# Hybrid decoder trunk: attention products with v in one task per head pair, residual norm on ScalarE, transposes of v and scores at other places in the weave

## The chip, the cores and the metric

The kernel runs on one core of one Trainium2 chip. The time is that of the whole program on the device, in microseconds (us). 2644.89 us is the median of three runs of the kernel before, which lie between 2642.65 and 2646.57.

## What is computed

Two layers over 2048 tokens of width 1024, all in float32. Each layer projects x at once into q, k, v, an attention gate, three gMLP parts and two branch gates. Attention is banded (128 keys before the query) with linear biases and a sink logit per head; the gMLP half normalises v_g and mixes it by position within chunks of 128.

```python
h = x @ w_in[l] + b_in[l]
q, k, v, z_a, u_g, v_g, z_g, g_a, g_g = split_columns(h)
y_a = sliding_window_attention(q, k, v, sinks[l]) * silu(z_a)
y_g = chunked_spatial_gating(gelu(u_g), gelu(v_g), ...) * silu(z_g)
merged = sigmoid(g_a) * (y_a @ w_branch_attn[l]) + sigmoid(g_g) * (y_g @ w_branch_gmlp[l])
x = layer_norm(ALPHA * x + merged @ w_out[l] + b_out[l], ln_g[l], ln_b[l])
```

There are 8 heads in 4 pairs; two heads of a pair share one 128-row tile, 64 rows each.

## The kernel before, in words

The work is cut into 2 layers x 4 groups of 512 tokens. `group(l, g, xs)` does one group of one layer. Its large products are 128x128 by 128x512, three for each block because every float32 operand is split into a rounded high part and a rest (`hilo`): high by high, high by rest, rest by high. A group has 1296 of them, all issued by the helper `mm` (L176). They come in units of 24: k, v, the four q tiles, four units for v_g, four for z_a, four for z_g, four for u, then the gates and branches, and last the output product.

Weights are split into high and rest in the first group of a layer only, by ScalarE (L135) and VectorE (L136), stored, and loaded as halves in the other groups.

Everything else is woven between these products. `side` is a queue of tasks, each a condition and an action. `step` counts the products and, each time `pace` of them have gone by, runs the task at the head if its condition holds; if it does not hold, it waits for another full `pace`:

```python
def step(w):
    count[0] += 1
    tick[0] += w
    while tick[0] >= pace[0]:
        tick[0] -= pace[0]
        if side and side[0][0]():
            side.popleft()[1]()
        else:
            tick[0] = 0.0
```

`pace` is 9 from the end of a group to the end of v_g (product 240), and 5 from there. The tasks of a group, in the order of the queue:

- `norm(b)`, four of them, left over from the group before (none for the first group): the residual norm of 128 rows as two instructions on VectorE (L645), two multiplications and additions by the norm's weights on GpSimd (L647, L648) and a store issued by GpSimd. In the very last group it runs another path, part of it on ScalarE (L637).
- a nop and four `v_task(r)`, appended after v's product, the 48th: each four transposes of 32x128 on VectorE (L346) that turn v into VT.
- 16 `s_task(c, b)`: scores of pair c and block b on TensorE (L375), bias and row maximum on VectorE (L383, L390), and after the fourth block the softmax (exponentials on ScalarE, L407; sums and scaling on VectorE, L409 to L412). The condition is that q's tile c is there and that 8 products have gone by since. q is evacuated in halves of 64 rows by ScalarE (L464) and VectorE (L465), k by L331 to L335.
- from product 240 on: `t_task(c, hf, r)`, 32 of them, each four transposes of the probabilities on VectorE (L425), and after the fourth two masks on GpSimd (L430, L432); between them 16 `pv_task(c, b)`, the products with v of one block (four products of 64 columns, eight instructions, L445). The fourth of a pair is followed by the multiplication with the gate (L451) and by `hilo` on ScalarE and VectorE. A product with v asks for 10 products since its masks were issued.
- statistics and norm of v_g (L511 to L520), mixing (L528 to L536), and in the second layer the turning of the next x (L287).

The program's order is a priority: within an engine the order of the instructions that comes out can differ from it, each instruction still waiting for what it needs. PSUM has five buffers for the large products and three for attention.

Of the kernel before, what the change touches and what calls it, by code (L numbers as in the profile page):

```python
# [10 lines left out]
AF = mybir.ActivationFunctionType  # L11
ALU = mybir.AluOpType
PSUM = bass.MemoryType.PSUM

P = 128
# [6 lines left out]
NB = T // P  # L22
HEADS = 8
NPAIR = HEADS // 2
HD = 64
# [10 lines left out]
PACE_E = 8.0  # L36
PACE_X = 8.0
T_DELAY = 45
P_DELAY = 10
LAG = 2  # L40
NEARLY = 5
# [7 lines left out]
def trunk_kernel(ctx, tc, xg, xt, wu, bcol, bvg, sinks, lngc, lnb, wsp, bsp, bout, ln_g, ln_b,  # L49
# [34 lines left out]
    def TT(shape=None):  # L84
        return tp.tile(shape or [P, T], F32, name=nm("t"), tag="t")
# [4 lines left out]
    def AT(shape=None):  # L90
        return ps_at.tile(shape or [P, T], F32, name=nm("at"), tag="at")

    def S(shape, tag):
        return small.tile(shape, F32, name=nm(tag), tag=tag)
# [57 lines left out]
    side = deque()  # L152
# [3 lines left out]
    count = [0]  # L156
# [41 lines left out]
    def hilo(dst, src, lo_engine=None):  # L198
        h, o = dst(), dst()
        act.copy(out=h, in_=src)  # L200
        (lo_engine or dve).tensor_tensor(out=o, in0=src, in1=f(h), op=ALU.subtract)
        return h, o
# [102 lines left out]
    def group(l, g, xs):  # L305
# [37 lines left out]
        def v_task(r):  # L343
            def go():
                for i in range(4):
                    dve.transpose(out=VT[32 * i:32 * i + 32, 1:, 32 * r:32 * r + 32],  # L346
                                  in_=v4[32 * r:32 * r + 32, :, 32 * i:32 * i + 32])
            return always, go
        side.append(nop)
        side.extend(v_task(r) for r in range(4))  # L350
        if l == 0 and g == 0:
            sp.dma_start(out=b8, in_=score_bias)
            pool.dma_start(out=vg_b, in_=bvg[l].partition_broadcast(P))
# [7 lines left out]
        q = {}  # L361
# [72 lines left out]
                due["p", c, hf] = count[0] + P_DELAY  # L434
            return (lambda: count[0] >= due["t", c]), go

        def pv_task(c, b):
            def go():
                A = att[c]
                if b == 0:  # L440
                    A["o"] = AT()
                po = A["o"]
                for kb in range(2):
                    for j in range(2):
                        pe.matmul(po[j * HD:(j + 1) * HD, b * P:(b + 1) * P],  # L445
                                  lhsT=VT[:, b + kb, j * HD:(j + 1) * HD],
                                  rhs=A["p"][b // 2][1 - kb][:, 2 * (b % 2) + j, :], start=kb == 0, stop=kb == 1,
                                  skip_group_check=True)
                if b == NB - 1:
                    y = TT()  # L450
                    dve.tensor_tensor(out=y, in0=po, in1=sza[c], op=ALU.mult)  # L451
                    ys[c] = hilo(Y, y)
                    del att[c]
            return (lambda: count[0] >= due["p", c, b // 2]), go

        side.extend(s_task(c, b) for c in range(NPAIR) for b in range(NB))
        pace[0] = PACE_S
        for c in range(NPAIR):
            ps = item()
            q_ = []  # L460
            for j in range(2):
                s, o = slice(j * HD, (j + 1) * HD), slice((1 - j) * HD, (2 - j) * HD)
                t = M()
                act.activation(out=t[s], in_=ps[s], func=AF.Identity, bias=bc[s, BQ + c:BQ + c + 1])  # L464
                dve.scalar_tensor_tensor(out=t[o], in0=ps[s], scalar=bc[s, BQ + c:BQ + c + 1],  # L465
                                         in1=f(t)[s], op0=ALU.add, op1=ALU.subtract)
                q_.append(t)
            q[c] = q_ + [count[0] + 8]


        hv = []
# [6 lines left out]
            hv.append(M(F32))  # L478
            dve.tensor_tensor(out=hv[b], in0=banks[b], in1=vg_b, op=ALU.add)
        flush(lambda: exps[0] == NPAIR)  # L480
        ready = []
        for c in range(NPAIR):
            for hf in range(2):
                for r in range(4):
                    side.append(t_task(c, hf, r))
                    if r % 2 and len(ready) > LAG:
                        side.append(ready.pop(0))
                ready += [pv_task(c, 2 * hf), pv_task(c, 2 * hf + 1)]
        for task in ready:
            side.extend([nop, task])  # L490
        pace[0] = PACE_T
        if l == 0 and g == 0:
            side.append(mix_consts(0))
# [110 lines left out]
        st = S([P, NB, 2, 6], "st2")  # L604
        mv = S([P, NB, 2], "mv2")
        rs = S([P, NB, 1], "rs2")
        last = l == DEPTH - 1 and g == NG - 1

        def stats(b, n):
            dve.tensor_scalar(out=rs[:, b:b + n, :], in0=mv[:, b:b + n, 1:2], scalar1=EPS, scalar2=None,  # L610
                              op0=ALU.add)
            pool.tensor_tensor(out=rs[:, b:b + n, :], in0=rs[:, b:b + n, :],  # L612
                               in1=mhalf[:, 0:n].unsqueeze(2), op=ALU.pow)

        def norm(b):
            row = g * NB + b
            dst = out[row * P:(row + 1) * P] if l == DEPTH - 1 else x1[g][:, b, :]
            if last:

                nmr = S([P, 1], "nmr")  # L620
                dve.scalar_tensor_tensor(out=nmr, in0=mv[:, b, 0:1], scalar=-1.0, in1=rs[:, b, :],
                                         op0=ALU.mult, op1=ALU.mult)
                own = [(T, D)] if b < NB - 2 else [(0, T), (T, T + 256)]
                rest = (0, T) if b < NB - 2 else (T + 256, D)

                def at(lo, hi):
                    return rt[b][lo // T][:, lo % T:(hi - 1) % T + 1], slice(lo, hi)
                for lo, hi in own:
                    r, cs = at(lo, hi)
                    dve.scalar_tensor_tensor(out=r, in0=r, scalar=mv[:, b, 0:1], in1=lg_b[:, cs],  # L630
                                             op0=ALU.subtract, op1=ALU.mult)
                for lo, hi in own:
                    r, cs = at(lo, hi)
                    dve.scalar_tensor_tensor(out=r, in0=r, scalar=rs[:, b, :], in1=lb_b[:, cs],
                                             op0=ALU.mult, op1=ALU.add)
                r, cs = at(*rest)
                act.activation(out=r, in_=r, func=AF.Identity, bias=nmr, scale=rs[:, b, :])  # L637
                pool.tensor_tensor(out=r, in0=r, in1=lg_b[:, cs], op=ALU.mult)  # L638
                pool.tensor_tensor(out=r, in0=r, in1=lb_b[:, cs], op=ALU.add)  # L639
                for h in range(2):  # L640
                    sp.dma_start(out=dst[:, h * T:(h + 1) * T], in_=rt[b][h])
                return
            for h in range(2):
                r, hs = rt[b][h], slice(h * T, (h + 1) * T)
                dve.tensor_scalar(out=r, in0=r, scalar1=mv[:, b, 0:1], scalar2=rs[:, b, :],  # L645
                                  op0=ALU.subtract, op1=ALU.mult)
                pool.tensor_tensor(out=r, in0=r, in1=lg_b[:, hs], op=ALU.mult)  # L647
                pool.tensor_tensor(out=r, in0=r, in1=lb_b[:, hs], op=ALU.add)  # L648
                pool.dma_start(out=dst[:, hs], in_=r)
# [34 lines left out]
        pace[0] = PACE_S  # L684
        if not last:
            stats(0, NB)
            side.extend((always, lambda b=b: norm(b)) for b in range(NB))
        return nxt

# [106 lines left out]
```

## Time and profile before

| | |
|---|---|
| runs | 2642.65, 2644.89, 2646.57 us, median 2644.89 |
| profiled execution | 2644.38 us, of which the span from the first to the last instruction is 2642.7 us |
| mean granted clock of TensorE | 0.989 of full speed |
| TensorE matmuls | 2579.4 us busy, 12176 instructions |
| VectorE | 1513.6 us busy, 3801 instructions |
| ScalarE | 650.2 us busy, 1266 instructions |
| GpSimd | 433.9 us busy, 448 instructions |

In the rows further down, PE is TensorE (PEld its weight loads), DVE is VectorE, ACT is ScalarE, POOL is GpSimd. L645 is line 645 of the kernel before. `y<-y,mv,rs` names the tile written and the tiles read. `x8` is a count. Busy time says how long an engine had an instruction in it; matmuls are pipelined, so that a single one's duration is longer than its distance to the next.

### The profile page before, as it was taken

What the parts mean: (1) busy time and instruction counts of PE and PEld (TensorE: products, weight loads), DVE (VectorE), ACT (ScalarE), POOL (GpSimd) and SP (SyncE); (2) the same over time, 40 slices, a digit from 0 to 9 for tenths busy, and PEclk for the clock granted to TensorE, in tenths of its full rate; (3) what the DMA queues carried; (4) which work ended last, traced back from release to release, by engine and by line L of the source; (5) the groups of instructions that cost most, each with busy time, mean ns of one, the idle gap of its engine ahead of it and who ended that gap; (6) DMA issues with size and microseconds to landing.
All of it is one profiled execution on the core that took longest, in us unless ns stands there. A gap on an engine that the chain in (4) does not pass through costs nothing. (4 is left out here: it accounts for less than half of the span.)

```text
span 2642.7 us, 32428 instructions
## 1 busy us (share of the span) xinstructions
PE 2579.4 (98%) x12176; PEld 2095.3 (79%) x12176; DVE 1513.6 (57%) x3801; ACT 650.2 (25%) x1266; POOL 433.9 (16%) x448
## 2 busy tenths in 40 slices
PE   8999999999999999999989999999999999999997
PEld 6788877888778887788877888778887788877886
DVE  7963478213782137824689577872467724676114
ACT  4432223211321113211144332321103211041110
POOL 1110031100311003110032100310013200121002
PEclk9999999999999999999999999999999999999999
DMA  8788954457544575456676897545665456644554
GB/s 320 238 288 291 336 208 160 165 196 260 177 159 175 192 256 189 164 187 224 249 253 207 299 322 285 177 159 189 214 228 179 161 187 211 228 173 157 181 197 164
DMA packets 116108, 568.39 MB, mean 215 GB/s; under 512 B 12112, under 2 KB 28528, under 8 KB 60528
## 3 DMA queue, kind: packets, MB, share of 16 engines
q1 hardware_dynamic: 109776, 546.35, 58.5%
q0 software_dynamic: 6176, 19.97, 2.2%
q8 instruction: 96, 1.57, 0.2%
q14 instruction: 60, 0.49, 0.1%
HBM read 436.25 MB, written 130.02 MB: 214 GB/s over the span
## 5 line engine op out<-in xcount | busy, mean ns | idle before, releaser
L176 PE MATMUL mm<-x,w 128*128 128x512 f32 x6528 | 1562.5, 396 | 10.1 <-ACT x L200 8.6
L176 PEld LDWEIGHTS mm<-x,w 128*128 128x128 f32 x6528 | 1221.5, 190 | 285.0 <-issue 21.9
L176 PE MATMUL mm<-y,w 128*128 128x512 f32 x1536 | 353.6, 389 | 0.0
L176 PE MATMUL mm<-w,m 128*128 128x512 f32 x1536 | 349.8, 389 | 0.2 <-DVE y L656 0.2
L176 PEld LDWEIGHTS mm<-w,m 128*128 128x128 f32 x1536 | 288.2, 188 | 60.5 <-DVE y L656 0.6
L176 PEld LDWEIGHTS mm<-y,w 128*128 128x128 f32 x1536 | 288.2, 188 | 59.8
L425 DVE STREAM_TRANSPOSE t<-t 32x128 f32<-32x128 f32 x1024 | 309.3, 302 | 13.9
L588 POOL TENSOR_TENSOR t<-t,t 128x512 f32<-128x512 f32 x64 | 84.8, 1325 | 992.4 <-DVE t L587 984.1
L136 DVE TENSOR_TENSOR w<-wr,w 128x1024 fp32r<-128x1024 f32 x108 | 146.9, 1360 | 139.0 <-ACT w L135 138.1
L584 DVE TENSOR_TENSOR t<-t,mm 128x512 f32<-128x512 f32 x64 | 43.7, 683 | 297.1 <-PE mm L176 297.0
L556 ACT ACTIVATE t<-mm,bcol 128x512 f32<-128x512 f32 x128 | 88.2, 689 | 457.1 <-PE mm L176 457.1
L176 PE MATMUL mm<-w,x 128*128 128x512 f32 x768 | 190.7, 392 | 0.0
L287 DVE STREAM_TRANSPOSE t<-t 32x128 f32<-32x128 f32 x512 | 154.8, 302 | 49.6 <-DMA t<-x 42.4
L135 ACT CAST w<-wr 128x1024 fp32r<-128x1024 f32 x108 | 113.2, 1048 | 199.1 <-DMA wr<-in_wu 100.1
L176 PEld LDWEIGHTS mm<-w,x 128*128 128x128 f32 x768 | 138.8, 189 | 25.3
L430 POOL TENSOR_SCALAR_AFFINE_SELECT t<-t 128x512 f32<-128x512 f32 x64 | 48.7, 762 | 616.0 <-DVE t L425 578.2
L383 DVE CUSTOM_DVE_ANT_0 t<-at,b 128x256 f32<-128x256 f32 (+1 forms) x256 | 97.5, 412 | 49.0 <-PE at L375 46.1
L407 ACT ACTIVATE t<-t,negm 128x128 f32<-128x128 f32 x256 | 99.3, 389 | 57.3 <-DVE negm L397 57.0
L656 DVE TENSOR_TENSOR y<-y,mm 128x512 f32<-128x512 f32 x64 | 43.8, 686 | 119.7 <-PE mm L176 119.7
L200 ACT CAST m<-t 128x512 fp32r<-128x512 f32 x64 | 39.7, 621 | 292.8 <-POOL t L588 292.8
L375 PE MATMUL at<-ka,m 128*128 128x256 f32 x256 | 71.0, 298 | 37.7 <-DVE m L465 37.7
L645 DVE TENSOR_SCALAR y<-y,mv,rs 128x512 f32<-128x512 f32 x56 | 88.8, 1655 | 8.0 <-POOL rs L612 8.0
(93 smaller groups left out, 1749.4 us busy)
## 6 DMA issues: line engine op xcount, KB each, us to landing
w<-kept SPq DMA_DIRECT2D x324, 1024.0 KB, 4.8
kept<-w SPq DMA_DIRECT2D x108, 1024.0 KB, 4.9
wr<-in_wu SPq DMA_DIRECT2D x108, 512.0 KB, 5.8
t<-in_xg SPq DMA_DIRECT2D x32, 256.0 KB, 6.3
y<-in_xt SPq DMA_DIRECT2D x32, 256.0 KB, 6.4
x<-y POOLq DMA_DIRECT2D x32, 256.0 KB, 3.3
t<-x SPq DMA_DIRECT2D x32, 256.0 KB, 5.5
y<-x SPq DMA_DIRECT2D x32, 256.0 KB, 6.3
```

The source lines that it names most:

```text
L135: act.copy(out=t[:, 0, :], in_=r)
L136: dve.tensor_tensor(out=t[:, 1, :], in0=r, in1=f(t)[:, 0, :], op=ALU.subtract)
L176: pe.matmul(o, lhsT=a, rhs=b, start=start, stop=stop, skip_group_check=skip)
L287: dve.transpose(out=outs[k][32 * i:32 * i + 32, :, 32 * r:32 * r + 32], in_=tiles[k][32 * r:32 * r + 32, :, 32 * i:32 * i + 32])
L375: pe.matmul(ps[:, j, :], lhsT=q[c][j][:, b * P:(b + 1) * P], rhs=KT[a][j][:, b * P:b * P + 2 * P], start=a == 0, stop=a == 1)
L383: dve.tensor_tensor_reduce(out=t[:, j, lo:], in0=ps[:, j, lo:], in1=b8[:, 2 * c + j, lo:], scale=1.0, scalar=NEG, op0=ALU.add, op1=ALU.max ...
L407: act.activation(out=w, in_=w, func=AF.Exp, bias=negm[:, bb, j:j + 1], scale=HD ** -0.5, accum_out=sums[:, bb, j:j + 1])
L425: dve.transpose(out=cur_[32 * i:32 * i + 32, :, 32 * r:32 * r + 32], in_=w[32 * r:32 * r + 32, :, 32 * i:32 * i + 32])
L430: pool.affine_select(out=prev_, in_=cur_, pattern=[[0, 4], [-1, P]], compare_op=ALU.is_gt, fill=0.0, base=0, channel_multiplier=1)
L556: act.activation(out=t, in_=ps, func=AF.Sigmoid, bias=bias(i))
L588: pool.tensor_tensor(out=sa, in0=sa, in1=sg, op=ALU.add)
L645: dve.tensor_scalar(out=r, in0=r, scalar1=mv[:, b, 0:1], scalar2=rs[:, b, :], op0=ALU.subtract, op1=ALU.mult)
```

## The change

The products with v of a head pair become one task of 16 products (32 instructions), which waits for the masks of the second half of the pair and stands after the third transpose task of the next pair; the last pair's stands after two nops. The four transpose tasks of v leave their place ahead of the scores and are appended after the v_g units, ahead of the transposes of the probabilities. The scores of a pair ask for 20 products since q's evacuation instead of 8. The residual norm becomes an activation on ScalarE with a scale and a bias per row; one more small VectorE instruction per group computes the bias (`nm4`). The last group's own norm path stays as it is.

```diff
--- before.py
+++ after.py
@@ -36,6 +36,7 @@
 PACE_E = 8.0
 PACE_X = 8.0
 T_DELAY = 45
+Q_DELAY = 20
 P_DELAY = 10
 LAG = 2
 NEARLY = 5
@@ -346,8 +347,6 @@
                     dve.transpose(out=VT[32 * i:32 * i + 32, 1:, 32 * r:32 * r + 32],
                                   in_=v4[32 * r:32 * r + 32, :, 32 * i:32 * i + 32])
             return always, go
-        side.append(nop)
-        side.extend(v_task(r) for r in range(4))
         if l == 0 and g == 0:
             sp.dma_start(out=b8, in_=score_bias)
             pool.dma_start(out=vg_b, in_=bvg[l].partition_broadcast(P))
@@ -434,24 +433,22 @@
                 due["p", c, hf] = count[0] + P_DELAY
             return (lambda: count[0] >= due["t", c]), go
 
-        def pv_task(c, b):
+        def pv_task(c):
             def go():
                 A = att[c]
-                if b == 0:
-                    A["o"] = AT()
-                po = A["o"]
-                for kb in range(2):
-                    for j in range(2):
-                        pe.matmul(po[j * HD:(j + 1) * HD, b * P:(b + 1) * P],
-                                  lhsT=VT[:, b + kb, j * HD:(j + 1) * HD],
-                                  rhs=A["p"][b // 2][1 - kb][:, 2 * (b % 2) + j, :], start=kb == 0, stop=kb == 1,
-                                  skip_group_check=True)
-                if b == NB - 1:
-                    y = TT()
-                    dve.tensor_tensor(out=y, in0=po, in1=sza[c], op=ALU.mult)
-                    ys[c] = hilo(Y, y)
-                    del att[c]
-            return (lambda: count[0] >= due["p", c, b // 2]), go
+                po = AT()
+                for b in range(NB):
+                    for kb in range(2):
+                        for j in range(2):
+                            pe.matmul(po[j * HD:(j + 1) * HD, b * P:(b + 1) * P],
+                                      lhsT=VT[:, b + kb, j * HD:(j + 1) * HD],
+                                      rhs=A["p"][b // 2][1 - kb][:, 2 * (b % 2) + j, :],
+                                      start=kb == 0, stop=kb == 1, skip_group_check=True)
+                y = TT()
+                dve.tensor_tensor(out=y, in0=po, in1=sza[c], op=ALU.mult)
+                ys[c] = hilo(Y, y)
+                del att[c]
+            return (lambda: count[0] >= due["p", c, 1]), go
 
         side.extend(s_task(c, b) for c in range(NPAIR) for b in range(NB))
         pace[0] = PACE_S
@@ -465,7 +462,7 @@
                 dve.scalar_tensor_tensor(out=t[o], in0=ps[s], scalar=bc[s, BQ + c:BQ + c + 1],
                                          in1=f(t)[s], op0=ALU.add, op1=ALU.subtract)
                 q_.append(t)
-            q[c] = q_ + [count[0] + 8]
+            q[c] = q_ + [count[0] + Q_DELAY]
 
 
         hv = []
@@ -478,16 +475,14 @@
             hv.append(M(F32))
             dve.tensor_tensor(out=hv[b], in0=banks[b], in1=vg_b, op=ALU.add)
         flush(lambda: exps[0] == NPAIR)
-        ready = []
+        side.extend(v_task(r) for r in range(4))
         for c in range(NPAIR):
             for hf in range(2):
                 for r in range(4):
                     side.append(t_task(c, hf, r))
-                    if r % 2 and len(ready) > LAG:
-                        side.append(ready.pop(0))
-                ready += [pv_task(c, 2 * hf), pv_task(c, 2 * hf + 1)]
-        for task in ready:
-            side.extend([nop, task])
+                    if c and hf * 4 + r == LAG:
+                        side.append(pv_task(c - 1))
+        side.extend([nop, nop, pv_task(NPAIR - 1)])
         pace[0] = PACE_T
         if l == 0 and g == 0:
             side.append(mix_consts(0))
@@ -604,6 +599,7 @@
         st = S([P, NB, 2, 6], "st2")
         mv = S([P, NB, 2], "mv2")
         rs = S([P, NB, 1], "rs2")
+        nm4 = S([P, NB, 1], "nm4")
         last = l == DEPTH - 1 and g == NG - 1
 
         def stats(b, n):
@@ -642,8 +638,7 @@
                 return
             for h in range(2):
                 r, hs = rt[b][h], slice(h * T, (h + 1) * T)
-                dve.tensor_scalar(out=r, in0=r, scalar1=mv[:, b, 0:1], scalar2=rs[:, b, :],
-                                  op0=ALU.subtract, op1=ALU.mult)
+                act.activation(out=r, in_=r, func=AF.Identity, bias=nm4[:, b, :], scale=rs[:, b, :])
                 pool.tensor_tensor(out=r, in0=r, in1=lg_b[:, hs], op=ALU.mult)
                 pool.tensor_tensor(out=r, in0=r, in1=lb_b[:, hs], op=ALU.add)
                 pool.dma_start(out=dst[:, hs], in_=r)
@@ -684,6 +679,7 @@
         pace[0] = PACE_S
         if not last:
             stats(0, NB)
+            dve.scalar_tensor_tensor(out=nm4, in0=mv[:, :, 0:1], scalar=-1.0, in1=rs, op0=ALU.mult, op1=ALU.mult)
             side.extend((always, lambda b=b: norm(b)) for b in range(NB))
         return nxt
```

## Rows read from the trace of the kernel before

**Rows 1.** The page: the span, and busy time of TensorE
```profile
span 2642.7 us, 32428 instructions
...
PE 2579.4 (98%) x12176; PEld 2095.3 (79%) x12176; DVE 1513.6 (57%) x3801; ACT 650.2 (25%) x1266; POOL 433.9 (16%) x448
```

**Rows 2.** List of waits, all of TensorE's: total us, times, longest
```profile
PE at L375 <- DVE m L465: 37.7, 14, 5.9
...
PE at L445 <- POOL t L432: 0.3, 1, 0.3
```

**Rows 3.** Timeline of the last boundary: start, length, engine, line, [idle before, releaser]
```profile
2300.56 22.60 PE L176 MATMUL mm<-x,w 128*128 128x512 f32 x99
...
2303.75 12.89 DVE L645 TENSOR_SCALAR y<-y,mv,rs 128x512 f32<-128x512 f32 x8 [1.13 <-POOL rs L612]
...
2306.20 0.69 ACT L331 ACTIVATE ka<-mm,bcol 64x512 fp32r<-64x512 f32 x1 [34.87 <-PE mm L176]
...
2316.57 0.73 DVE L333 SCALAR_TENSOR_TENSOR kb<-mm,bcol,ka 64x512 fp32r<-64x512 f32 x1
...
2321.05 5.05 DVE L346 STREAM_TRANSPOSE vt<-t 32x128 f32<-32x128 f32 x16
...
2326.13 0.74 DVE L465 SCALAR_TENSOR_TENSOR m<-mm,bcol,m 64x512 fp32r<-64x512 f32 x1
...
2326.93 0.38 PE L375 MATMUL at<-ka,m 128*128 128x256 f32 x1 [3.77 <-DVE m L465]
...
2328.44 0.58 PE L375 MATMUL at<-ka,m 128*128 128x256 f32 x1 [1.00 <-DVE m L465]
...
2329.03 4.04 PE L176 MATMUL mm<-x,w 128*128 128x512 f32 x9
```

**Rows 4.** Windows at boundaries: PE, PEld, DVE, ACT, POOL busy (count), granted clock, DMA share
```profile
1011.00:1026.00 15.00, 10.25 (x45) 8.16 (x44) 10.59 (x31) 2.73 (x4) 6.81 (x8) 0.89 0.47 148
1337.00:1352.00 15.00, 6.45 (x22) 4.89 (x22) 13.45 (x26) 4.14 (x5) 10.44 (x12) 0.66 0.98 330
...
2322.90:2337.90 15.00, 10.23 (x39) 8.20 (x38) 9.65 (x30) 2.57 (x4) 6.61 (x8) 0.77 0.41 140
```

**Rows 5.** Groups of instructions: busy us, mean ns of one | idle before
```profile
L645 DVE TENSOR_SCALAR y<-y,mv,rs 128x512 f32<-128x512 f32 x56 | 88.8, 1655 | 8.0 <-POOL rs L612 8.0
...
L445 PE MATMUL at<-t,vt 128*64 128x128 f32 x1024 | 84.4, 285 | 0.3 <-POOL t L432 0.3
...
L511 DVE BATCH_NORM_STATS2 st<-m 128x6 f32<-128x512 f32 x32 | 21.3, 669 | 0.2
...
L520 DVE TENSOR_SCALAR m<-m,mv,rs 128x512 f32<-128x512 f32 x32 | 15.9, 561 | 9.0 <-POOL rs L515 9.0
...
L637 ACT ACTIVATE y<-y,nmr,rs 128x512 f32<-128x512 f32 x2 | 1.6, 818 | 35.7 <-DVE nmr L621 35.7
```

**Rows 6.** Line L326: ns min/median/max, first and last start in us
```profile
L326 DVE CAST ka<-ka x12: 216/220/227, 70.5 to 2034.4; 128x128 fp32r<-128x128 f32 x12
```

**Rows 7.** Timeline of TensorE among the products with v, ordinary group
```profile
2399.10 0.66 PE L445 MATMUL at<-t,vt 128*64 128x128 f32 x8
2399.69 3.74 PE L176 MATMUL mm<-x,w 128*128 128x512 f32 x15
2403.36 0.66 PE L445 MATMUL at<-t,vt 128*64 128x128 f32 x8
```

**Rows 8.** Timeline: last operand and last second half, ordinary and first group
```profile
2424.87 0.63 POOL L432 TENSOR_SCALAR_AFFINE_SELECT t<-t 128x512 f32<-128x512 f32 x1
...
2438.20 0.66 PE L445 MATMUL at<-t,vt 128*64 128x128 f32 x8
...
1455.15 0.67 POOL L432 TENSOR_SCALAR_AFFINE_SELECT t<-t 128x512 f32<-128x512 f32 x1
...
1456.16 0.66 PE L445 MATMUL at<-t,vt 128*64 128x128 f32 x8
```

**Rows 9.** Window from v_g's last product to the last with v, first group
```profile
1389.10:1460.20 71.10, 71.10 (x384) 53.08 (x383) 66.97 (x176) 29.52 (x48) 19.74 (x19) 1.00 0.64 222
```

## The prediction

> **What bounds the kernel now.** I read the page first. TensorE is busy 2579.4 of 2642.7 us [rows 1], so only three things can move the time: the stretches where TensorE stands, the stretches where it runs at a low clock, and the time that its own instructions take. The profiled execution took 2644.38 us against a median of 2644.89 for the runs shown; my sum starts from 2644.4. A difference of 0.2% (5.3 us) is about what a measurement of this kernel can tell from no change.
>
> The list of waits shows where TensorE stands: 37.7 us, 14 times, in front of the first score products (L375), released by VectorE's L465, the second half of q [rows 2]. Its products with v waited 0.3 us in all [rows 2]. The timeline of the last of the seven boundaries between groups shows how that wait arises [rows 3]. The group's products start at 2300.56. VectorE has the eight residual norms L645 from 2303.75 to 2316.64, while the sum for k, done at about 2306.2, waits for its second pass on VectorE (L333, at 2316.57). Then come k, 16 transposes of v (L346) until 2326.10, and only then q's second half at 2326.13. TensorE has run out of products ahead of the scores and stands 3.77 us, then 1.00 for the second head. After it, nine products take 4.04 us where 99 had taken 22.60.
>
> The windows of 15 us around the boundaries show the second part of the price: a granted clock of 0.77 in five of them, 0.89 and 0.66 in the others [rows 4]; they mix the levels of 2.4 and 1.2 GHz. The shortfall is 15 x (5 x 0.23 + 0.11 + 0.34) = 24 us. About 1.4 us per boundary of the low stretch is idle time counted already, half of which comes off: 24 - 5 = 19. The boundary costs 37.7 + 19, say 56 us, 8 per boundary.
>
> **The change, part by part.**
>
> *The norm.* Removed from VectorE: 56 instructions of 1655 ns, 12.9 us per boundary; put on ScalarE as 56 activations, plus one small VectorE instruction (nm4, about 0.2 us, in a place where VectorE waits anyway). The nearest row for the activation is L637, the same one in the last group, four times, 820 to 600 ns, 128x512 at 818 [rows 5]. ScalarE had been idle 34.87 us before L331 at 2306.20 [rows 3], so from about 2304 it takes 8 x 0.82 = 6.5 us, until 2310.5, and k's evacuation, queued behind on ScalarE, starts 4.3 us later than now. Its steps, two of 0.69 on ScalarE and two of 0.75 on VectorE for each head, end at 2316.3. q's product is the 72nd, ended at 2300.56 + 72 x 0.228 = 2317.0, and takes 2.9 us to evacuate: 2319.9. The scores come after 99 products, at 2323.1. So there are 3 us to spare. GpSimd's multiplications, which follow the norm, and its stores keep their length and are waited for by nobody on this path.
>
> The row shows 1655 ns for the norm on VectorE; the same operation at the same shape took 561 in L520 [rows 5]. The Trainium skill, ScalarE: Activation LUTs, section Rules for kernel authors, says to put adds and multiplications on VectorE and not on ScalarE. By L520's duration that is right, 4.5 us against 6.5 per boundary, and the move would cost 2 us; by L645's own row it frees 12.9 for 6.5, and I go by that row.
>
> *v behind the scores, and the delay of 20.* In program order the first scores do not move. Before: one task per 9 products, four norms at 9 to 36, nothing at 45, a nop at 54, the v tasks at 63 to 90, scores at 99, which is the x99 of the timeline [rows 3]. After: the scores are at the head from 48 on but refused until 72 + 20 = 92, so the next tick, 99, takes them. Without the delay they would stand at 81. The transposes are another matter: each engine's order is not the program's. L326, the first lines of a group, ran from 70.5 us on, inside the group before [rows 6]; what is ready and finds its engine idle runs early. The v transposes are ready when v is, as now, and VectorE is idle then, so most likely they stay in front of q: 2316.3 + 5.05 = 2321.4, first head of q 2322.1, second 2323.5. That is a wait of 0.4 us at most, for the second head. With the weights split by VectorE and ScalarE (boundary into the second layer, clock 0.66 [rows 4]) there is less room; I leave 4 us for it. Gain of the boundary: 56 - 4 = 52. Bounds: 46 (1.4 us of wait at each of the others) and 58 (only 1.0 us of idle time in each low stretch).
>
> *Products with v.* Now 128 bursts of eight instructions. From one burst's start to the next are 4.26 us with 15 products between [rows 7], so a burst costs 4.26 - 15 x 0.228 = 0.84. Its eight instructions last 0.66 [rows 7] and one of them 0.285 [rows 5]; they start two at a time, one for each head, so three steps lie in 0.66 - 0.285, 0.125 each. The rest of the 0.84 is entering and leaving, paid once for four bursts in one: 0.84 + 12 x 0.125 = 2.34 instead of 3.36, a gain of 1.02 per pair and 33 us for 32 pairs. If the 24 added instructions take the mean of the burst, 0.66 / 8 each, it is 2.82, and 17 us. I take 1.0 per pair, 32 us: the step is the nearer row, and nothing in the burst shows a shorter one, so 33 is the upper bound.
>
> *What the products with v then wait for.* Tasks come every 5 products after product 240: the four-burst tasks stand at 314, 359, 404 and 444, where the second halves stood at 319, 379, 439 and 484. For the last pair that is 40 products earlier (9.1 us), and 14 bursts of 0.84 ahead of it become three of 2.34 (4.7 us): 13.8 us in all. In an ordinary group it began at 2438.20 and its operand was ready at 2425.50 [rows 8]: it would come at 2424.4 and wait 1.1. In the first group of a layer it began at 1456.16, ready at 1455.82 [rows 8]: it would come at 1442.4 and wait 13.5. There VectorE has no room: 66.97 of 71.1 us busy [rows 9]. Part of that can step aside: statistics and norm of the gMLP half, four of 669, four of 561 and small ones, about 5.8 us [rows 5], are not needed yet. So 0 to 13.5 us in each of two groups; I take 8 (13.5 - 5.8, rounded up). In the six others 0 to 1.1; I take 1. Together 16 + 6 = 22 us given back. Queued behind a waiting product on TensorE is everything, so it counts in full.
>
> The sum: 52 + 32 - 22 = 62, so 2644.4 - 62 = 2582 us. Its own bounds: 58 + 33 - 0 = 91, 2553; and 46 + 17 - 27 - 7 - 7 (the last a clock drop of 3.5 in each first group) = 22, 2622.
>
> **The rivals.**
>
> *The order gives way.* If the products with v are issued later wherever their operand is late, nothing is given back: 52 + 32 = 84, 2560 us. For it: engines run out of program order [rows 6]. Against: in the first group of a layer the bursts with v kept their places though the margin was down to 0.3 us [rows 8].
>
> *The wait moves to ScalarE.* If an activation next to GpSimd takes the 1655 ns that VectorE took, k waits until 2317, q until about 2328, and the boundary stays as it is: 2644.4 - 32 + 22 = 2634. Against: L637 at 0.82 [rows 5], and no row in which ScalarE is lengthened as VectorE is.
>
> *Slower: v really lands behind the scores.* Its 16 transposes (5.05 us) then stand in front of the first p transposes on VectorE, in every group. Every wait above grows by 5: 6.2 us in six groups and 18.6 in two, and each is as long as those that brought the low clock, about 3 us. 6 x 9.2 + 2 x 21.6 = 98, against 56 + 32 = 88: 2654. It decides once the waits exceed 11 us a group. For it: the program's order says so. Against: VectorE stands idle at v's moment.
>
> *The weave does nothing* is true of the scores, as counted; it costs and gives nothing and is in every case.
>
> **How the numbers follow.** Forecast with its part given back 0.57, order gives way 0.25, wait on ScalarE 0.08, slower 0.05, and 0.05 for no wait removed and no cheaper burst, near 2645 on either side. The range reaches from the second case's good end, 2553, to just inside the forecast's bad one, 2618; outside lie the ScalarE and the slower case and slivers. Faster by over 0.2%: 0.57 + 0.25 + 0.08 + 0.03 = 0.93; within 0.02; slower 0.05.
>
> **What would show it.** Right: the wait of L375 for L465 under 5 us in all; windows at the boundaries at a clock of 1.00; eight activations in a row on ScalarE where L645 was, of 0.6 to 0.82; bursts of 32 instructions of about 2.3 us, 32 of them; waits of L445 for GpSimd's L432 in the first group of each layer, some 8 us, and little elsewhere. Wrong: v's transposes found between the last softmax and the first p transposes; bursts in two pieces; TensorE still waiting for L465; or activations of over a microsecond. If L445's waits exceed 11 us per group, the sign is wrong.

## The result, and the profile after

The changed kernel takes 2601.03 us, the median of four runs (2599.18 to 2603.85), against 2644.83 for four runs of the kernel before beside it: a ratio of 0.9836 (0.9819 to 0.9853). The forecast was 2582 in a range of 2553 to 2618, so sign and range hold, and of the 62 us forecast 44 came. The profiled execution is the run of 2599.18 us, 45.2 less than the one of before. The edit moves lines: the large product is L177, the scores L374, the second half of q L462, the products with v L443, the transposes of the probabilities L424, the masks L429 and L431, the transposes of v L347, the norm L641, the gate's multiplication L448.

The page of the changed kernel, which answers [rows 1]:

```profile
span 2597.5 us, 32421 instructions
...
PE 2538.0 (98%) x12176; PEld 2100.9 (81%) x12176; DVE 1445.7 (56%) x3752; ACT 690.0 (27%) x1322; POOL 431.8 (17%) x448
```

VectorE lost the 56 norms that ScalarE gained. TensorE's share is 98% in both kernels: the share doesn't tell where 45 us went. The list of TensorE's waits does; it answers [rows 2] (total us, times, longest):

```profile
PE at L443 <- POOL t L429: 28.7, 13, 6.0
...
PE at L443 <- POOL t L431: 4.8, 13, 1.1
...
PE at L374 <- DVE m L462: 1.6, 1, 1.6
```

The wait in front of the scores has gone, from 37.7 us to 1.6. A new one has come: the products with v, which waited 0.3 us before, now wait 33.5 us for the masks of the probabilities.

The timeline of the last boundary answers [rows 3]:

```profile
2264.04 22.60 PE L177 MATMUL mm<-x,w 128*128 128x512 f32 x99
...
2267.50 3.64 ACT L641 ACTIVATE y<-y,nm,rs 128x512 f32<-128x512 f32 x5 [32.69 <-DVE nm L682]
...
2271.04 0.67 ACT L332 ACTIVATE ka<-mm,bcol 64x512 fp32r<-64x512 f32 x1
...
2272.44 2.23 ACT L641 ACTIVATE y<-y,nm,rs 128x512 f32<-128x512 f32 x3
...
2277.65 5.05 DVE L347 STREAM_TRANSPOSE vt<-t 32x128 f32<-32x128 f32 x16
...
2282.74 0.74 DVE L462 SCALAR_TENSOR_TENSOR m<-mm,bcol,m 64x512 fp32r<-64x512 f32 x1
...
2286.48 0.28 PE L374 MATMUL at<-ka,m 128*128 128x256 f32 x1
...
2286.95 2.23 PE L177 MATMUL mm<-x,w 128*128 128x512 f32 x9
```

ScalarE does five norms, then the first two passes of k, then the other three. k's evacuation starts 7.0 us after the group's first product (2271.04 - 2264.04). The transposes of v run before q, though the program now has them behind the scores. q's first head is done at 2283.5, three us before the scores at 2286.48. The scores come after 99 products, as before, without a wait, and the nine products behind them take 2.23 us where they took 4.04 at the low clock.

Three windows at boundaries (busy time of PE, PEld, DVE, ACT and POOL, then the granted clock), which answer [rows 4]:

```profile
1060.00:1075.00 15.00, 12.71 (x75) 10.10 (x73) 13.41 (x39) 1.21 (x2) 3.61 (x5) 0.97 0.33 126
1315.00:1330.00 15.00, 13.30 (x57) 10.53 (x56) 14.51 (x30) 4.20 (x6) 14.91 (x14) 0.89 0.98 354
2279.00:2294.00 15.00, 15.00 (x73) 12.63 (x72) 12.17 (x31) 3.43 (x5) 14.17 (x15) 1.00 0.79 267
```

The last is the boundary of the timeline, at the full clock. The second is the boundary into the second layer, the one place where the scores still wait, and the clock falls to its low level (1.2 GHz) for a part of it. The first lies in an ordinary group and at no boundary: it ends behind a wait of the products with v. The groups of the norm and of the products with v answer [rows 5] (busy us, mean ns of one | idle before, by releaser):

```profile
L641 ACT ACTIVATE y<-y,nm,rs 128x512 f32<-128x512 f32 x56 | 41.2, 806 | 184.2 <-DVE nm L682 184.0
...
L443 PE MATMUL at<-t,vt 128*64 128x128 f32 x1024 | 73.4, 289 | 33.7 <-POOL t L429 28.7 <-POOL t L431 4.8
```

**Where the 45 us come from.** I cut each of the eight groups at TensorE's product starts: the first product, product 240 and product 494 (between these two lies the stretch of the products with v), and the next group; in the last group the rest is counted to eight products before its end. Summed over the groups, in us, for all kernels of this study:

| | 0 to 240 | 240 to 494 | rest |
|---|---|---|---|
| before | 565.7 | 568.0 | 1485.5 |
| after | 510.3 | 581.0 | 1482.9 |
| e1, the norm alone | 507.4 | 572.5 | 1485.5 |
| e2, all but the norm | 566.6 | 580.2 | 1482.9 |
| e3, the weave undone | 509.0 | 586.9 | 1482.9 |
| e4, products with v later | 511.6 | 542.7 | 1482.9 |
| e5, y from the other pool | 509.5 | 551.8 | 1483.0 |
| e6, e4 and wider first groups | 508.9 | 528.3 | 1494.2 |
| e7, e4 and e5 | 508.5 | 541.6 | 1482.9 |
| e8, e4 and weights on GpSimd | 511.1 | 548.6 | 1483.0 |

The first stretch, that of the boundaries, gave 55.4 (565.7 - 510.3). Of these, 1.2 lie in the program's first group, which no boundary precedes (70.9 before, 69.7 after; 69.4 to 71.0 over the kernels of the table); the seven boundaries gave 54.2. The stretch of the products with v, which should have become shorter, became 13.0 longer. The rest gave 2.6. Together 45.0.

The timeline of the last group, an ordinary one, shows the first and the second pair's products with v and what the second's wait for:

```profile
2343.31 1.97 PE L443 MATMUL at<-t,vt 128*64 128x128 f32 x32
2345.20 10.49 PE L177 MATMUL mm<-x,w 128*128 128x512 f32 x45
...
2346.36 1.25 DVE L506 BATCH_NORM_STATS2 st<-m 128x6 f32<-128x512 f32 x2
...
2349.19 2.54 DVE L515 TENSOR_SCALAR m<-m,mv,rs 128x512 f32<-128x512 f32 x4 [1.15 <-POOL rs L510]
...
2351.65 0.68 DVE L448 TENSOR_TENSOR t<-at,m 128x512 f32<-128x512 f32 x1
2352.25 1.24 DVE L424 STREAM_TRANSPOSE t<-t 32x128 f32<-32x128 f32 x4
...
2355.63 1.09 PE L443 MATMUL at<-t,vt 128*64 128x128 f32 x16
2358.10 0.64 POOL L429 TENSOR_SCALAR_AFFINE_SELECT t<-t 128x512 f32<-128x512 f32 x1 [7.56 <-DVE t L424]
2358.79 0.44 PE L443 MATMUL at<-t,vt 128*64 128x128 f32 x4 [2.07 <-POOL t L429]
...
2359.49 0.88 PE L443 MATMUL at<-t,vt 128*64 128x128 f32 x12 [0.26 <-POOL t L431]
```

Read it from the bottom. The second half of the second pair arrives on TensorE at about 2356.7, stands 2.07 us for the mask L429 and 0.26 for L431. GpSimd had been idle 7.56 us before that mask: it waited for VectorE's transposes. And VectorE did not start those until 2352.25, because statistics and norm of the gMLP half (from 2346.27) and the gate's multiplication of the first pair (L448, 2351.65) came first. So it is in all six ordinary groups: these instructions stand between the transposes of the second pair's first and second half. In the first group of a layer the same wait is longer, at the last pair (first layer):

```profile
136.90 1.09 PE L443 MATMUL at<-t,vt 128*64 128x128 f32 x16
...
142.30 1.62 POOL L429 TENSOR_SCALAR_AFFINE_SELECT t<-t 128x512 f32<-128x512 f32 x1 [7.58 <-DVE t L424]
...
143.97 0.69 PE L443 MATMUL at<-t,vt 128*64 128x128 f32 x4 [5.98 <-POOL t L429]
...
145.54 1.55 PE L443 MATMUL at<-t,vt 128*64 128x128 f32 x12 [0.88 <-POOL t L431]
```

The twelve instructions that took 0.88 us in the ordinary group take 1.55 here: the clock is at its low level after the wait. Ahead of the longest wait of each first group (this one, and 4.9 us at the third pair in the second layer) the norm L515 and the gate's multiplication stand in front of the late transposes as well.

### The profile page after: what moved, and what is told of

It reads as the page before. It is cut to its first block, busy times and chain, and to the rows that moved or that the text cites. A ratio compares the mean times of both kernels' runs of the same rounds, so it can differ in the third digit from the quotient of the medians.

```text
span 2597.5 us, 32421 instructions
## 1 busy us (share of the span) xinstructions
PE 2538.0 (98%) x12176; PEld 2100.9 (81%) x12176; DVE 1445.7 (56%) x3752; ACT 690.0 (27%) x1322; POOL 431.8 (17%) x448
## 3 DMA queue, kind: packets, MB, share of 16 engines
q8 instruction: 96, 1.57, 0.2%
## 4 chain that ended last, share of the span: by engine, by line
PE 76%; DVE 13%; issue 6%; POOL 3%; DMA 1%; ACT 1%; POOLq 0%; SPq 0%; DVEq 0%; ACTq 0%
PE mm L177 72%; DVE t L424 5%; PE at L374 2%; PE at L443 1%; PE at L523 1%; DVE t L288 1%; DVE w L137 1%; DMA wr<-in_wu 1%; DVE t L411 1%; DVE m L515 1%; POOL t L429 1%; DVE t L382 1%; ACT t L406 1%; POOL t L431 0%; DVE st L506 0%
## 5 line engine op out<-in xcount | busy, mean ns | idle before, releaser
L177 PE MATMUL mm<-x,w 128*128 128x512 f32 x6528 | 1525.9, 393 | 8.9 <-ACT x L201 6.3
L177 PEld LDWEIGHTS mm<-x,w 128*128 128x128 f32 x6528 | 1225.9, 189 | 268.5 <-issue 6.4
L177 PE MATMUL mm<-y,w 128*128 128x512 f32 x1536 | 353.6, 389 | 0.0
L177 PE MATMUL mm<-w,m 128*128 128x512 f32 x1536 | 349.8, 389 | 0.2 <-DVE y L651 0.2
L177 PEld LDWEIGHTS mm<-w,m 128*128 128x128 f32 x1536 | 288.3, 188 | 60.4 <-DVE y L651 0.6
L177 PEld LDWEIGHTS mm<-y,w 128*128 128x128 f32 x1536 | 288.3, 188 | 59.7
L424 DVE STREAM_TRANSPOSE t<-t 32x128 f32<-32x128 f32 x1024 | 309.4, 302 | 14.0
L137 DVE TENSOR_TENSOR w<-wr,w 128x1024 fp32r<-128x1024 f32 x108 | 146.5, 1359 | 149.0 <-ACT w L136 146.5
L579 DVE TENSOR_TENSOR t<-t,mm 128x512 f32<-128x512 f32 x64 | 43.6, 682 | 313.2 <-PE mm L177 313.1
L177 PE MATMUL mm<-w,x 128*128 128x512 f32 x768 | 190.8, 392 | 0.0
L177 PEld LDWEIGHTS mm<-w,x 128*128 128x128 f32 x768 | 138.8, 189 | 25.3
L429 POOL TENSOR_SCALAR_AFFINE_SELECT t<-t 128x512 f32<-128x512 f32 x64 | 45.6, 713 | 528.0 <-DVE t L424 517.2
L651 DVE TENSOR_TENSOR y<-y,mm 128x512 f32<-128x512 f32 x64 | 43.8, 686 | 120.5 <-PE mm L177 120.5
L443 PE MATMUL at<-t,vt 128*64 128x128 f32 x1024 | 73.4, 289 | 33.7 <-POOL t L429 28.7
L201 ACT CAST y<-t 128x512 fp32r<-128x512 f32 x64 | 39.7, 620 | 246.6 <-DVE t L448 191.4
```

Source lines behind the costliest of these rows:

```text
L137: dve.tensor_tensor(out=t[:, 1, :], in0=r, in1=f(t)[:, 0, :], op=ALU.subtract)
L177: pe.matmul(o, lhsT=a, rhs=b, start=start, stop=stop, skip_group_check=skip)
L424: dve.transpose(out=cur_[32 * i:32 * i + 32, :, 32 * r:32 * r + 32], in_=w[32 * r:32 * r + 32, :, 32 * i:32 * i + 32])
L429: pool.affine_select(out=prev_, in_=cur_, pattern=[[0, 4], [-1, P]], compare_op=ALU.is_gt, fill=0.0, base=0, channel_multiplier=1)
L443: pe.matmul(po[j * HD:(j + 1) * HD, b * P:(b + 1) * P], lhsT=VT[:, b + kb, j * HD:(j + 1) * HD], rhs=A["p"][b // 2][1 - kb][:, 2 * (b % 2) ...
```

## The experiments

**e1: the norm alone.** The kernel before, with nothing but the norm moved:

```diff
-                dve.tensor_scalar(out=r, in0=r, scalar1=mv[:, b, 0:1], scalar2=rs[:, b, :],
-                                  op0=ALU.subtract, op1=ALU.mult)
+                act.activation(out=r, in_=r, func=AF.Identity, bias=nm4[:, b, :], scale=rs[:, b, :])
...
+            dve.scalar_tensor_tensor(out=nm4, in0=mv[:, :, 0:1], scalar=-1.0, in1=rs, op0=ALU.mult, op1=ALU.mult)
```

> The kernel before with one edit: the residual norm on ScalarE (with its small nm4 on VectorE); products with v, v's transposes and the delay of 8 as before. Theory A, the whole boundary gain (55 us between the two traces, products 0 to 240) comes from the norm alone: about 2590 us (2584 to 2596), TensorE's waits for q at the first scores under 4 us, v's transposes still ahead of q. Rival B, v's transposes and the delay have a part in it: above 2605 us and waits of over 10 us left.

Measured: 2590.6 us (2588.7 to 2592.23), ratio 0.9795 (0.9781 to 0.981). TensorE's waits at the scores (L375, as in the kernel before) and at the products with v (L445):

```profile
PE at L445 <- POOL t L430: 2.0, 1, 2.0
...
PE at L375 <- DVE m L465: 0.8, 1, 0.8
```

The norm alone removes the boundary's wait and its low clock, 58.2 us of the first stretch (565.69 - 507.45), and is 10.4 us faster than the whole change.

**e2: everything but the norm.** The same edit backwards, on the changed kernel.

> The changed kernel with the norm back on VectorE, everything else changed. Theory A, the remaining parts lose by themselves: merged products with v save 38 us in their bursts and give back more than that in waits for the masks, so 2601 + 55 = 2656 us (2648 to 2662), with the old waits for q of some 35 to 40 us in front of the first scores. Rival B, the merging gains: 2645 or less.

Measured: 2655.28 us (2653.97 to 2656.33), ratio 1.004 (1.0025 to 1.0055). TensorE's waits:

```profile
PE at L374 <- DVE m L462: 38.2, 14, 5.6
PE at L443 <- POOL t L429: 26.9, 13, 4.4
```

Without the norm's move the wait at the scores is back in full, and the rest of the change loses 10.8 us. The two parts add up: e1 gains 53.9, e2 loses 10.8, the whole gains 43.8. So the merged products with v, as they are placed, cost more than they save.

**e3: the weave undone.** v's transposes and the delay as before, norm and merged products as in the change.

```diff
-Q_DELAY = 20
+Q_DELAY = 8
...
+        side.append(nop)
+        side.extend(v_task(r) for r in range(4))
...
-        side.extend(v_task(r) for r in range(4))
+        side.extend([nop] * 4)
```

> The changed kernel with v's transposes back ahead of the scores, the delay back at 8 and four empty tasks where v's transposes stood, so that every other task keeps its place. Theory A, these two parts cancel and v's transposes ran ahead of q in any case: 2601 us within 4, first scores still after 99 products. Rival B, the later place relieves VectorE: 2610 us or more, and TensorE waiting for q again.

Measured: 2603.57 us (2600.58 to 2604.14), ratio 0.9841 (0.9824 to 0.9857), against 0.9836 for the change: no difference that the intervals tell apart. In the timeline v's transposes run from 2282.54 to 2287.6, 13.6 us after the group's first product, and in the change 13.6 us after it too (2277.65 - 2264.04). Where the program names them made no difference to the time. Within it, two stretches moved against each other: at the boundary into the second layer TensorE waits 0.8 us for q, where the change waits 1.7, and that stretch is 2.6 us shorter (63.6 against 66.2); the stretches of the products with v are 5.9 us longer, 5.1 of it from 41.0 us at the low clock against 30.7. The profiled execution is the slowest of e3's four.

**e4: the merged products later.** On the changed kernel, the task of a pair 20 products later and the last one 20 later too:

```diff
-LAG = 2
+LAG = 6
...
-        side.extend([nop, nop, pv_task(NPAIR - 1)])
+        side.extend([nop] * 6 + [pv_task(NPAIR - 1)])
```

> The changed kernel with each merged product with v four tasks (20 products) later, behind the seventh instead of the third transpose task of the next pair, the last one behind six empty tasks instead of two. Theory A, the waits come from the place: the transposes of the next pair's second half then stand ahead of the multiplication with the gate, the 2.3 us wait of the second pair in the six ordinary groups goes (with its clock drop some 14 us in all), and the first groups of a layer wait 4 to 5 us less each: 2577 us (2570 to 2584). Rival B, VectorE has too much to do and the waits move along: 2595 us or more.

Measured: 2562.19 us (2560.86 to 2563.11, three runs), ratio 0.9688 (0.9671 to 0.9704). Waits at the products with v:

```profile
PE at L443 <- POOL t L429: 7.0, 4, 2.5
...
PE at L443 <- POOL t L431: 2.6, 5, 1.3
```

This is below the range that I had expected (2570 to 2584): 39 us are gained by the place alone. The stretch falls from 581.0 to 542.7. Each of the six ordinary groups takes 66.05 us in it, with no wait; after took 66.9 to 70.4, before 71.0 in most. The first groups of the layers fall from 84.3 and 81.3 to 72.5 and 73.9, by 11.9 and 7.4, where I had allowed 4 to 5 each.

**e5: the gate's result in another pool.** The changed kernel's order and places, but y takes its buffer from another pool than the transposed probabilities:

```diff
-                y = TT()
+                y = M(F32)
```

> The changed kernel with one edit: the product of attention and gate (y) takes its buffer from the pool of the gates instead of the pool that the transposes' tiles come from; every task keeps its place. Theory A, the ordinary groups' wait comes from that pool handing out buffers in the program's order, so that the next pair's second transposes queue behind y and the gMLP norm slips in front of them: in this kernel's order they run before y, the wait of the second pair in the six ordinary groups goes, 2601 - 14 = 2587 us (2582 to 2592), the first groups of a layer little changed. Rival B, the merged tasks simply come too early for VectorE whatever the order: 2597 us or more, with the ordinary groups' wait still there.

Measured: 2568.89 us (2566.66 to 2570.3), ratio 0.9714 (0.9696 to 0.9731). The timeline of VectorE in the last group, in the time that answers to the one shown of after:

```profile
2321.41 5.03 DVE L424 STREAM_TRANSPOSE t<-t 32x128 f32<-32x128 f32 x16
...
2327.15 1.23 DVE L424 STREAM_TRANSPOSE t<-t 32x128 f32<-32x128 f32 x4
2328.41 0.69 DVE L448 TENSOR_TENSOR m<-at,m 128x512 f32<-128x512 f32 x1
2329.14 1.25 DVE L424 STREAM_TRANSPOSE t<-t 32x128 f32<-32x128 f32 x4
...
2344.00 1.01 DVE L515 TENSOR_SCALAR m<-m,mv,rs 128x512 f32<-128x512 f32 x1
```

and TensorE behind it:

```profile
2330.09 1.97 PE L443 MATMUL at<-t,vt 128*64 128x128 f32 x32
2331.99 10.49 PE L177 MATMUL mm<-x,w 128*128 128x512 f32 x45
2342.41 1.97 PE L443 MATMUL at<-t,vt 128*64 128x128 f32 x32
```

One word of an allocation is worth 32 us. The next pair's transposes now start before the gate's multiplication, the gMLP norm (L515) comes only at 2344.00, behind them, and the second pair's 32 products run in one piece. The wait in ordinary groups was one of order on VectorE, not of its load. That tiles of one pool are handed out in the order of the program, so that the next p tiles could not come in front of y's, fits this and the edit, but it is argued from them: no run showed the handing out itself, and none separates it from the rival that the pool was merely one buffer short (y no longer takes one of its 15). The time lies 13 us below the lower end that I had expected (2582). The ordinary groups gave 19 us, where I had put 14, and my expectation that the first groups would hardly change was wrong: they fell to 79.7 and 75.8.

**e6: e4, with wider first groups.** One more empty task after each half in the first group of each layer:

```diff
+                if g == 0:
+                    side.append(nop)
```

> The kernel with the products with v four tasks later, and in the first group of a layer alone one more empty task behind every half pair (eight in all, 40 products by the last). Theory A, what is left there is VectorE being full, with the splitting of the weights beside the transposes: waits for the masks fall from 9.6 us to under 2, and the time from 2562.7 by some 8 to 14 us (with the clock) to 2552 (2547 to 2556). Rival B, the waits move along with the place because VectorE is paced by TensorE's progress through the weights: 2560 us or more.

Measured: 2556.06 us (2555.44 to 2559.26), ratio 0.9669 (0.9654 to 0.9684), the fastest of the study, 45 us below the change. TensorE's waits:

```profile
PE mm L177 <- DVE w L137: 4.8, 6, 1.7
PE at L443 <- POOL t L431: 2.3, 2, 1.1
...
PE at L443 <- POOL t L429: 1.4, 2, 0.8
```

The waits for masks are down to 3.7 us, from 9.6 in e4; I had expected under 2, and 2552 us. What is late next is the splitting of the weights (L137), which VectorE does in the first group of each layer. The table shows it as 11.3 us more in the rest, of which about 4 are two bursts moved beyond product 494; I did not pursue the others.

**e7: e4 and e5 together.**

> The products with v four tasks later and y's buffer from the pool of the gates, both at once. Theory A, the two edits cure the same wait (the queueing behind y), and nothing is left of it in the ordinary groups: within 4 us of the 2562.7 of the later place alone. Rival B, the buffers also hold up the first group of a layer: 2556 us or less.

Measured: 2560.31 us (2558.19 to 2561.58), ratio 0.9687 (0.967 to 0.9704). That is e4's time: the two edits cure the same wait, and the second has nothing left to cure.

**e8: e4, with weights split on GpSimd.** To relieve VectorE in the first groups, 12 of the 54 subtractions of each layer go to GpSimd:

```diff
-            dve.tensor_tensor(out=t[:, 1, :], in0=r, in1=f(t)[:, 0, :], op=ALU.subtract)
+            (pool if cur[0] % NUNITS in range(10, 22) else dve).tensor_tensor(out=t[:, 1, :], in0=r, in1=f(t)[:, 0, :], op=ALU.subtract)
```

> The products with v four tasks later, and in the first group of a layer the rest of twelve weight units (the unit of the first z_a tile and the eleven behind it) computed on GpSimd instead of VectorE: 12 x 1.36 us off VectorE, some 12 x 2.6 us (twice a 512-column multiplication) onto GpSimd, among the masks. Theory A, VectorE being full is what the first groups' products with v wait for: waits for the masks from 9.6 us to under 4, 2562.7 - 6 to - 12, 2551 to 2557. Rival B, the masks themselves or the weights come late when GpSimd takes the rests: 2561 us or more, with waits for GpSimd's L429 or for the weights.

Measured: 2567.77 us (2566.15 to 2568.43), ratio 0.9713 (0.9697 to 0.9728), 5.6 us slower than e4, where I had expected a gain; the waits for masks are 11.3 us, against 9.6. A stretch of the first group in e8, VectorE's softmax scaling and GpSimd beside it:

```profile
91.09 4.75 POOL L137 TENSOR_TENSOR w<-wr,w 128x1024 fp32r<-128x1024 f32 x2 [0.81 <-ACT w L136]
...
91.53 5.58 DVE L411 TENSOR_SCALAR t<-t,rinv 128x128 f32<-128x128 f32 x8
```

and the same eight instructions in e4, with GpSimd idle but for the last 0.4 us of a mask:

```profile
88.03 1.85 DVE L411 TENSOR_SCALAR t<-t,rinv 128x128 f32<-128x128 f32 x8
```

The scaling takes three times as long while GpSimd subtracts. VectorE is as busy as in e4 (1441.3 us against 1441.4): the subtractions that it lost had taken 28 us, of which 10 came back in the scaling (53.3 us busy in e4, 63.5 here), 9 in the `hilo` subtractions of y (L202, 45.9 and 54.5) and the rest in smaller groups. My rival, that the masks come late because GpSimd subtracts, can hold at one mask in each first group, the second pair's, which starts right behind other work of GpSimd; at the other late ones GpSimd stood idle until VectorE's transposes were done. A subtraction took 2393 ns on GpSimd and 1359 on VectorE in the changed kernel.

## Why the prediction was right and where it was wrong

**The boundary, forecast 52, measured 55.4: right, by its mechanism.** (The seven boundaries alone gave 54.2.) The norm took 806 ns on ScalarE (forecast 820). k came out at 7.0 us into the group and not behind all eight norms, because ScalarE took k after five; I had queued it behind eight. q's first head was ready three us before the scores and the second 1.5 (2285.00), and TensorE came without a wait at all but the boundary into the second layer (1.6 us of wait; that stretch takes 66.2 where the other boundaries take 62.4, so the 4 us that I had left for wait and clock were right). My bounds of 46 and 58 were added up wrongly: 58 leaves out these 4, and 1.4 us at each of the six others, as I wrote, gives 43.6. The forecast does not use them; the good end of the range does and would be 2557. e1 and e2 show that the norm alone does it. The rival that put the wait on ScalarE fell with the 806 ns. By the Trainium skill, ScalarE: Activation LUTs, section Rules for kernel authors, additions and multiplications belong on VectorE; here the same operation took 1655 ns on VectorE beside GpSimd (e2 has it again, 1655), so the measurement decided against that rule, by the row that I went by.

**v behind the scores, and the delay, forecast 0: right.** The transposes ran in front of q as before, and e3 shows that the weave is worth nothing measurable. With that the slower rival fell. The first scores at 99 products came as counted. The rival in which the weave does nothing was true, and cost nothing.

**Merging the products with v, forecast 32, measured 39: right, a little small.** An ordinary stretch of 240 to 494 takes 66.05 us without waits (e4, e5) and took 70.9 in the mean before: 4.85 per group, 1.2 per pair where I had taken 1.0. Eight times 4.85 is 39. The burst of 32 lasts 1.97 us, and one of its instructions 0.273 (the median), so its fifteen steps of two are 0.113 each, below the 0.125 that I had read from the short bursts; my upper bound of 33 was none.

**What the products then wait for, forecast 22, measured 52: this is the step that failed.** With 39 gained and 13.0 lost in the stretch, 52 were given back. Even the bad end of my sum allowed only 41 (27 + 7 + 7). The listed waits are 33.5 of these. The pieces at the low clock in these stretches are 30.7 us long, of which half, 15, is lost (some 2 of it while TensorE waits anyway). The rest, 3 to 5 us, I put down to the cuts in the bursts; no run measures it alone. Bursts in pieces were one of my signs of being wrong: 14 of the 32 came so, with the wait between a pair's first and second half, all eight in the first groups and one in each ordinary group. I had the mechanism (products earlier, operands not) and mis-sized it in three ways.

- *The pair.* I counted the margin of the last pair alone and found 1.1 us in an ordinary group. The wait fell on the second, whose task had moved from product 379 to 359: VectorE is held there by the gMLP half and the gate, 6 us in front of its transposes. Five of the six ordinary groups waited about 2.3 us, and one 0.4, where the task came six products later (at 365). The six gave back 19 us, where I took 6.
- *What steps aside.* I let 5.8 us of statistics and norm "step aside", since they are not needed yet. The timeline has them in front. An engine's order is not the program's, as I had said of v, but the same order stood in every ordinary group, late operand or not. e5 shows what it costs: with the order turned, the ordinary wait is gone. The first groups gave back 17.6 and 15.0 us (84.3 and 81.3 against 66.7 and 66.3, their time before less 4.85), 12.4 and 9.4 of it in waits and 5.1 each by the clock, where I took 8 each out of 0 to 13.5.
- *The clock.* I charged no fall of the clock for these waits, though [rows 4] showed what waits of a few us cost at the boundaries; it stood only in the bad end of the range. It came in both first groups and in three ordinary ones.

The sum by measured terms: 55.4 + 39 - 52 + 2.6 = 45. The rival "the order gives way" fell: tasks stayed at products 314, 359, 404 and 444 and waited in place. e4 is what that rival would have been had the program said so, and it took 2562 where the rival forecast 2560. That they agree is partly luck: e4 still gave back 13 us in the first groups (72.5 and 73.9 against 66.7 and 66.3), and the boundaries, the bursts and the rest gave 12 more than the rival's 84.

So the merged products are worth their 39 us only where their operands are ready; e6, with nearly no wait for masks, comes to 2556, 3 us above the good end of my range.

## What to carry to other kernels

When work on a bound engine is made shorter and moved earlier, check the margin of every operand it waits for, not of the last one, and read the order of the engine that makes the operand: what stands in front there will not step aside. A change with several parts is worth taking apart even when it wins: here the norm alone beat the whole, and the losing part became worth 35 us (2590.6 to 2556.1) by moving it a few tasks. Before relieving one engine through another, look at how long the first one's instructions last while the other works.

## What the runs showed of the hardware

**The same wait does not always cost the clock.** Three windows of 10 us from about the end of the second pair's wait, in groups 2, 3 and 7 of the changed kernel (counted from 0), and TensorE behind that wait in the first two:

```profile
757.50:767.50 10.00, 9.82 (x52) 8.06 (x52) 9.59 (x30) 2.00 (x3) 1.40 (x3) 1.00 0.50 164
1073.00:1083.00 10.00, 9.12 (x44) 7.26 (x45) 9.57 (x30) 1.76 (x3) 2.47 (x4) 0.83 0.31 105
2358.00:2368.00 10.00, 8.95 (x43) 7.04 (x44) 9.53 (x31) 1.43 (x3) 2.54 (x4) 0.83 0.32 107
...
756.98 0.44 PE L443 MATMUL at<-t,vt 128*64 128x128 f32 x4 [2.03 <-POOL t L429]
757.68 0.88 PE L443 MATMUL at<-t,vt 128*64 128x128 f32 x12 [0.26 <-POOL t L431]
...
1073.62 0.44 PE L443 MATMUL at<-t,vt 128*64 128x128 f32 x4 [2.03 <-POOL t L429]
1074.33 1.55 PE L443 MATMUL at<-t,vt 128*64 128x128 f32 x12 [0.26 <-POOL t L431]
```

TensorE waited 2.03 and 0.26 us in the first two and 2.07 and 0.26 in the third, after the same instructions. The clock stayed at 1.00 in the first and fell to its low level, 1.2 GHz, for a part of the other two; the stretch from product 240 to 494 took 68.8 us in the first, 70.2 and 70.4 in the others. The boundary into the second layer shows it across kernels: the change and e4 to e8 all wait 1.57 us there for the second head of q, and the clock fell in three of the six (the change, e4, e8: that stretch took 66.2) and not in the others (64.6 to 64.7). What decides between them is open.

**VectorE's instructions lengthen beside GpSimd, but not all of them.** In the kernel before, the norm took 1655 ns in the mean, and [rows 5] has 561 for the same operation in another place. Within that line, the 14 of the 56 that no multiplication or addition on GpSimd overlapped took 575 ns in the mean, the 42 others 2015. e8 made the same happen to the softmax's scaling, 1.85 to 5.58 us for eight. There the two-input subtractions of L202 lengthened as well, from 689 ns to 1467 where a two-input instruction of GpSimd overlapped them, while VectorE's transposes (L424) took 302 either way. The Trainium skill, GPSIMD Engine Reference, section 1. Specifications, says that the two engines share their SBUF interfaces and that the contention strikes VectorE's instructions in a 2-port mode or with two SBUF inputs. The traces agree that VectorE is slowed there, the two-input L202 among others, and add the size, a factor of three for the one-input scaling; whether the one-input instructions run in such a mode is shown by no run here.
